# A transformer-like layer step in one kernel: the norm ahead of the feed-forward takes its scale and bias after the turn

## The chip, the cores and the metric

One core of one Trainium2 chip runs the whole layer as one program. The metric is the device time of that program in microseconds (us). The core has a matrix engine (PE in the profile, its weight loads PEld), a vector engine (DVE), a scalar engine (ACT), a general engine (POOL) and a queue engine for transfers (SP). Each runs its own list of instructions in the listed order; an instruction that waits holds all that stand behind it on its engine.

## The reference

One layer on 640 rows (512 prompt rows and 8 x 16 rows of running streams), width 1024. What matters here is its second half: the merged branches go through `w_out`, a norm follows, then a gated feed-forward of width 2816, then a second norm. Everything is fp32.

```python
def layer_norm(x, g, b):
    mu = x.mean(-1, keepdims=True)
    var = jnp.square(x - mu).mean(-1, keepdims=True)
    return (x - mu) * lax.rsqrt(var + LN_EPS) * g + b

z = x @ w_in                      # 1024 -> 6656: branch inputs, query, and three sigmoid gates
...                               # branches A (recurrence), B (conv), C (attention)
merged = g[:, :, 0] * out_a + g[:, :, 1] * out_b + g[:, :, 2] * out_c
x = layer_norm(DEEPNORM_ALPHA * x + merged @ w_out, ln1_g, ln1_b)
ffn = (jax.nn.silu(x @ w_ffn_gate) * (x @ w_ffn_up)) @ w_ffn_down
x = layer_norm(DEEPNORM_ALPHA * x + ffn, ln2_g, ln2_b)
```

## The kernel before, in words

**Split products.** Every fp32 operand of a matmul is kept as a high and a low part (fp32r). ACT copies the high part (`copy`), DVE subtracts it for the low part, and three matmuls (high x high, high x low, low x high) make one product. A row of activations is held turned, 128 features on the partitions and 640 tokens along the row: `xh` and `xl`, 8 blocks of 128 features each. A matmul of 128x320 takes half of the tokens (`HT` = 320, c = 0 or 1), so one full block column costs 8 x 3 x 2 matmuls.

**Order.** The program is a list of `Step`s, one for each weight block, in the order in which PE works through them. For a step, `prep_hi` (ACT) and `prep_lo` (DVE) prepare its weights two to four steps ahead, in the buffers `wh` and `wl` (three each), from `wr` (two buffers of 1 MB, filled by SP). Other work is written as generators ("streams"). A planner (`advance`) adds prices of instructions up per engine and lets a stream issue its next piece whenever DVE and ACT are behind PE by these prices; `finish` forces a stream to its end. `flush` issues the evacuation of the step before. All of this happens when the program is built: what comes out is one fixed order per engine.

**Seven products instead of eight.** The three gates and the feed-forward (except its first 256 columns) are made with Strassen's scheme in Winograd's form, over pairs of column blocks: `seven` issues m1, m4, m2, m6, m5, m7, m3 for the first pair (`first=True`). m1, m2 and m4 read quarters of `xh`/`xl` themselves; m6, m5, m7 and m3 read sums of quarters, s2, s1, s3, s4 in that order. `sums_stream` makes them: it first rebuilds whole fp32 quarters, `xh + xl` (8 adds of 128x640 on DVE in all), mixes them (8 adds or subtractions), and splits each sum in a high and a low part (8 copies on ACT, 8 subtractions on DVE). Its order is s2, s3, s1, s4 for the feed-forward. For the gates s1 comes last and overwrites a quarter of `xh`/`xl`. m2 adds to the PSUM tile of m1, so it cannot start before ACT has copied m1 out. Ahead of m1 of the first pair, `sums_there` issues everything of the sums that is still left.

**w_out and the norm.** `wo_tile` multiplies tiles of 128 tokens (t = 0 to 4), tiles 0 and 1 together, then 2, 3, 4, each 8 x 6 matmuls of 128x512. `wo_evac` then adds the residual (DVE) and starts a stream `x1_t`:

```python
def x1_stream(t):
    yield from ln_rows(res[t], gb["1"][0], gb["1"][1])
    ...                      # the finished rows go to the DRAM scratch x1, for the second residual
    yield from to_xt(t, res[t])
```

`ln_rows` takes the statistics (two BN_STATS), has POOL make the root `rs`, and applies mean, gain, root and bias with four DVE passes of 128x512 per tile. The gain and bias are broadcast over 128 partitions (`gb["1"]`, four 256 KB loads). `to_xt` turns the tile on PE (8 transposes into a PSUM tile `pv`), and ACT and DVE split it from PSUM into `xh` and `xl`.

**Feed-forward start.** Its first 256 columns (gate g and up u, two blocks each) are a `group`: PE first does the c = 0 halves of g0, g1, u0, for which tiles 0, 1 and half of 2 are enough, then `x1_done` forces the streams of the norm to their end and starts the stream of the sums; then come the c = 1 halves, then u1, then the first pair.

**Down.** `before_down` loads the rows of x1 back (`xres`, in the place of `xh`) and the second norm's gain and bias (`gb2`, in the place of `xl`) on POOL's queue. `w_ffn_down` is multiplied for tiles 0 to 2 in 22 steps, then for tiles 3 and 4 in a second round.

## Time and profile before

| what | value |
|---|---|
| runs | 1071.85, 1073.41, 1075.06 us (median 1073.41) |
| profiled execution | 1074.25 us, of it span 1072.1 us |
| mean granted clock of the matrix engine | 0.991 |
| PE busy, share of the span | 1047.4 us, 98% |
| DVE, ACT, POOL busy | 798.8, 469.1, 89.5 us |

All arithmetic on DVE, ACT and PE is recorded by one helper, so its line is always L64; groups are told apart by the names of tiles. `s` is any of the 128x640 slots in SBUF, `pu` and `pv` are PSUM tiles, `x` is the scratch of x1 rows. In a timeline a row gives start, duration, engine, what it writes and reads, and in brackets how long the engine was idle before it and what released it. Matmuls overlap: one of 128x320 is shown with about 310 ns, but the next starts 147 ns later.

### The profile page before, as it was taken

Reading aid. Unit: us, or ns where it says so; the run is one execution under the profiler, and the core shown is the slowest. Engines: PE = TensorE matmul, PEld = TensorE weight load, DVE = VectorE, ACT = ScalarE, POOL = GpSimd, SP = SyncE. Lnnn points to the kernel's source line nnn. Section 1 sums busy time; section 2 is a strip of 40 time slices with the busy share of each in tenths; the row PEclk is TensorE's granted clock in tenths of the full one; section 3 lists DMA queues with packets and bytes.
Section 4 is the critical chain, followed back from the end, with each engine's and each line's share of the span. In section 5 each row is a group of like instructions: output and inputs, shape, how many; then the busy total and the mean of one; then the engine's idle time right before and its main releaser. Section 6 shows DMA issues by size and latency. Waiting matters only on the chain.

```text
span 1072.1 us, 16734 instructions
## 1 busy us (share of the span) xinstructions
PE 1047.4 (98%) x6745; PEld 998.4 (93%) x6745; DVE 798.8 (75%) x1357; ACT 469.1 (44%) x823; POOL 89.5 (8%) x142
## 2 busy tenths in 40 slices
PE   9899999999999999999999998999999999999997
PEld 8799899999999999999998898999999999888886
DVE  7939889799676645989654688888878887544775
ACT  5322655254675438565332024343444444344341
POOL 0100304322100000000001310000000000100111
PEclk9899999999999999999999999999999999999999
DMA  9722126532122122212335321222222222733471
GB/s 346 280 87 80 48 86 209 186 106 79 40 79 79 60 79 79 79 45 80 118 105 193 112 102 40 79 79 82 108 87 80 79 80 85 288 137 139 172 279 40
DMA packets 28541, 123.63 MB, mean 115 GB/s; under 512 B 3728, under 2 KB 4560, under 8 KB 18608
## 3 DMA queue, kind: packets, MB, share of 16 engines
q1 hardware_dynamic: 21744, 100.62, 26.3%
q0 software_dynamic: 6720, 21.94, 6.0%
q8 instruction: 53, 0.87, 0.3%
q14 instruction: 24, 0.20, 0.1%
HBM read 112.67 MB, written 9.88 MB: 114 GB/s over the span
## 4 chain that ended last, share of the span: by engine, by line
PE 83%; DVE 10%; DMA 3%; ACT 2%; issue 1%; POOL 0%; SPq 0%; DVEq 0%; POOLq 0%; ACTq 0%
PE pu L64 74%; PE pv L64 10%; DVE s L64 7%; DVE wl L64 2%; ACT s L64 1%; DMA s<-in_w_mem_k 1%; DMA pb<-in_rows_b 1%; DMA s<-in_x_prompt 1%; DMA s<-in_w_mem_v 1%; DVE xres L64 0%; DVE xl L64 0%; ACT L64 0%; DVE mx L64 0%; POOL s L777 0%; DVE nm L64 0%
## 5 line engine op out<-in xcount | busy, mean ns | idle before, releaser
L64 PE MATMUL pu<-xh,wh 128*128 128x320 f32 x1040 | 251.7, 314 | 8.3 <-ACT s L64 7.5
L64 PE MATMUL pu<-xh,wl 128*128 128x320 f32 x1040 | 247.6, 310 | 0.0
L64 ACT ACTIVATE wh<-wr 128x1024 fp32r<-128x1024 f32 (+1 forms) x149 | 135.1, 908 | 242.2 <-PE pu L64 152.4
L64 PE MATMUL pu<-xl,wh 128*128 128x320 f32 x888 | 220.6, 312 | 4.2 <-DVE xl L64 4.2
L64 PEld LDWEIGHTS pu<-xh,wh 128*128 128x128 f32 x1040 | 178.8, 190 | 12.9 <-ACT s L64 9.2
L64 PE MATMUL pu<-s,wh 128*128 128x320 f32 x1064 | 185.6, 310 | 1.7 <-DVE s L64 1.3
L64 DVE TENSOR_TENSOR s<-s,s 128x640 fp32r<-128x640 f32 (+4 forms) x180 | 129.0, 732 | 67.3 <-ACT s L64 60.7
L64 PEld LDWEIGHTS pu<-xh,wl 128*128 128x128 f32 x1040 | 178.2, 189 | 0.0
L64 DVE TENSOR_TENSOR wl<-wr,wh 128x1024 fp32r<-128x1024 f32 (+1 forms) x113 | 129.9, 1151 | 62.9 <-ACT wh L64 62.7
L64 PEld LDWEIGHTS pu<-s,wh 128*128 128x128 f32 x1064 | 163.1, 188 | 3.3 <-ACT wh L64 1.1
L64 PEld LDWEIGHTS pu<-xl,wh 128*128 128x128 f32 x888 | 155.1, 190 | 4.8 <-DVE xl L64 4.7
L64 PE MATMUL pu<-s,wl 128*128 128x320 f32 x808 | 148.1, 311 | 0.2 <-DVE s L64 0.2
L64 DVE TENSOR_TENSOR s<-s,pu 128x320 f32<-128x320 f32 x188 | 88.5, 485 | 75.0 <-PE pu L64 71.4
L64 ACT ACTIVATE s<-s 128x640 fp32r<-128x640 f32 (+4 forms) x148 | 89.8, 627 | 99.0 <-DVE s L64 97.6
L64 PEld LDWEIGHTS pu<-s,wl 128*128 128x128 f32 x808 | 126.8, 190 | 0.5 <-ACT wh L64 0.5
L64 DVE SCALAR_TENSOR_TENSOR s<-s,pb,s 128x511 f32<-128x511 f32 (+14 forms) x240 | 114.5, 549 | 9.5 <-ACT s L64 9.4
L64 PE MATMUL pu<-wh,s 128*128 128x512 f32 (+1 forms) x396 | 114.8, 383 | 0.0
L64 PEld LDWEIGHTS pu<-wh,s 128*128 128x128 f32 x396 | 72.8, 188 | 13.9
L64 ACT ACTIVATE s<-pu 128x320 f32<-128x320 f32 (+2 forms) x90 | 36.6, 441 | 71.9 <-PE pu L64 71.9
L64 PE MATMUL pu<-wl,s 128*128 128x512 f32 (+1 forms) x198 | 61.6, 383 | 0.4 <-DVE wl L64 0.4
L64 PE MATMUL pv<-wh,s 128*128 128x512 f32 (+1 forms) x152 | 48.7, 367 | 0.4 <-DVE xres L64 0.4
L64 PE MATMUL pu<-s,s 128*128 128x512 f32 (+1 forms) x204 | 46.6, 380 | 0.0
(125 smaller groups left out, 1115.9 us busy)
## 6 DMA issues: line engine op xcount, KB each, us to landing
wr<-in_w_in SPq DMA_DIRECT2D x26, 1024.0 KB, 4.8
wr<-in_w_ffn_down SPq DMA_DIRECT2D x19, 1024.0 KB, 4.8
wr<-in_w_ffn_gate SPq DMA_DIRECT2D x11, 1024.0 KB, 4.8
wr<-in_w_ffn_up SPq DMA_DIRECT2D x11, 1024.0 KB, 4.8
s<-in_cache_k POOLq DMA_DIRECT2D x16, 256.0 KB, 5.2
s<-in_cache_v POOLq DMA_DIRECT2D x16, 256.0 KB, 4.9
wr<-in_proj_a SPq DMA_DIRECT2D x4, 1024.0 KB, 4.8
wr<-in_w_out SPq DMA_DIRECT2D x4, 1024.0 KB, 6.2
```

Source lines behind the costliest of these rows:

```text
L64: return f(*a, **k)
```

## The change: what it does

Mean and root of the norm are still applied to the rows. ACT does it with two passes per tile (scale `rs`, bias `shift`); for the last tile DVE takes one of the two. The rows in x1 are therefore without gain and bias. The tile is then turned, and gain and bias are applied as the eviction from PSUM, where they are one number per partition (columns 43 and 44 of `pa`, which is loaded at the start): half of the blocks on ACT, half on DVE. The result goes into fp32 tiles `whole_x` in SBUF, and `turn_parts` splits it from there into `xh` and `xl`. The `whole_x` tiles are handed to `sums_stream` (`given`), which does not rebuild quarters any more. For the second residual `scale_stream` applies gain and bias to the rows after they are loaded back, with ten DVE passes of 128x1024 at fixed steps of the down stage; `gb2` has two more loads.

The pieces of the norm are no stream any more: `x1_jobs` is a table that names after which matmul group (tile or group, number) each piece is issued. The sums for the feed-forward come in the order s2, s1, s3, s4, and `sums_for` forces, ahead of each product that reads a sum, only what is needed for that one, for the gates too.

```diff
-    it = one.tile([128, 128], I32, name="it")
+    it = get([128, 128], I32)
...
-    def sums_there():
+    def sums_for(n):
         flush()
         for item in list(streams):
             if item[0][:4] == "sums":
-                for _ in item[1]:
-                    pass
-                streams.remove(item)
+                while n not in made:
+                    next(item[1], None)
...
         def whole(n, i):
             t0, k0 = QUARTERS[n]
+            if given is not None:
+                a[n, i] = given.pop((t0 // HT, (k0 + i) // 2))
+                return
...
-        yield from part("s3", "21")
         if in_place is None:
             yield from part("s1", "22")
+        yield from part("s3", "21")
...
-            if first and i == 0:
-                before = sums_there
+            if first and xn[0] == "s":
+                before = lambda xn=xn: sums_for(xn)
...
+    def x1_sum(t):
+        residual(t, wo_acc.pop(t))
+        x1_norm[t] = ln_stats(res[t])
+
+    def x1_scale(t):
+        y = res[t]
+        mv, ve, rs = x1_norm.pop(t)
+        if t < 4:
+            ln_scale(y, mv, rs)
+        else:
+            V.tensor_scalar(y[0], y[0], mv[:, 0:1], rs, op0=OP.subtract, op1=OP.mult)
+            ln_scale(y[1:], mv, rs)
...                                   # both halves of the rows go to the scratch x1 on POOL's queue
+    def x1_gain(t, half):
...
+                    if half:
+                        V.tensor_scalar(w[:, e], src, pa[:, k, 43:44], pa[:, k, 44:45], op0=OP.mult, op1=OP.add)
+                    else:
+                        A.activation(w[:, e], src, AF.Identity, scale=pa[:, k, 43:44], bias=pa[:, k, 44:45])
...
+               (3, 5): [(x1_turn, 2)], (3, 6): [(x1_gain, 2, 0)],
+               (4, 0): [(x1_sum, 3), (x1_gain, 2, 1)], (4, 1): [(x1_scale, 3), (x1_split, 2)], (4, 4): [(x1_turn, 3)],
+               (4, 5): [(x1_gain, 3, 0), (x1_gain, 3, 1), (x1_split, 3)],
+               (5, 0): [(x1_sum, 4), (x1_scale, 4)], (5, 7): [(x1_turn, 4)],
+               (5, 8): [(x1_gain, 4, 0), (x1_gain, 4, 1), (x1_split, 4)]}
...
+    def turn_parts(t, i):
+        for c, a, b in pieces(t):
+            w = whole_x[c, i][:, :, a - c * HT:b - c * HT]
+            copy(xh[:, 2 * i:2 * i + 2, a:b], w)
+            V.tensor_sub(xl[:, 2 * i:2 * i + 2, a:b], w, f32(xh[:, 2 * i:2 * i + 2, a:b]))
...
+        for i, z in ((2, ln1_g), (3, ln1_b), (0, ln2_g), (1, ln2_b)):
...
+        def scale_stream():
+            for t in range(5):
+                for i, op in ((2, OP.mult), (3, OP.add)):
+                    while state["i"] < first["down"] + 2 * t + i + 4:
+                        yield None
+                    V.tensor_tensor(r[:, t], r[:, t], g[:, i], op=op)
+                    yield 1
```

One more slot is there (53), and the rotation of slot numbers shifts by it everywhere. PE has the same matmuls and 40 transposes; four of the five tiles are now turned before the feed-forward begins, not three.

**DVE from the residual of tile 3 on** (SCALAR_TENSOR_TENSOR with `pu` is the residual, `wl` are low parts of the weights of g0 and g1, `s_378_6480` and its like after the change are `whole_x` tiles). Before, from the second half of the residual of tile 3 to the first half of that of tile 4:

```order
L64 SCALAR_TENSOR_TENSOR s_371_6334<-s_371_6334,pu 128x512
L64 TENSOR_TENSOR wl<-wr,wh 128x1024 x2
L64 TENSOR_TENSOR xl<-pv,xh 128x4x128 x2
L64 BN_STATS st<-s_370_6333 128x6
L64 BN_STATS st<-s_371_6334 128x6
L64 BN_AGGR mv<-st 128x2
L64 TENSOR_SCALAR ve<-mv 128x1
L64 SCALAR_TENSOR_TENSOR s_370_6333<-s_370_6333,mv,s_352_6074 128x512
L64 SCALAR_TENSOR_TENSOR s_371_6334<-s_371_6334,mv,s_353_6075 128x512
L64 SCALAR_TENSOR_TENSOR s_370_6333<-s_370_6333,rs,s_354_6078 128x512
L64 SCALAR_TENSOR_TENSOR s_371_6334<-s_371_6334,rs,s_355_6079 128x512
L64 SCALAR_TENSOR_TENSOR s_372_6430<-s_372_6430,pu 128x512
```

After, from the statistics of tile 3 to its shift, and then from the weights to the residual of tile 4:

```order
L64 BN_AGGR mv<-st 128x2
L64 TENSOR_SCALAR ve<-mv 128x1
L64 TENSOR_SCALAR s_369_6315<-pv,pa 128x64 x2
L64 TENSOR_SCALAR s_377_6475<-pv,pa 128x64 x2
L64 TENSOR_SCALAR s_370_6318<-pv,pa 128x64 x2
L64 TENSOR_SCALAR s_378_6480<-pv,pa 128x64 x2
L64 SCALAR_TENSOR_TENSOR shift<-mv,rs 128x1
```

```order
L64 TENSOR_TENSOR wl<-wr,wh 128x1024 x2
L64 TENSOR_SCALAR s_377_6475<-pv,pa 128x128 x2
L64 TENSOR_SCALAR s_378_6480<-pv,pa 128x128 x2
L64 TENSOR_TENSOR xl<-s_373_6436,xh 128x2x128
L64 TENSOR_TENSOR xl<-s_374_6441,xh 128x2x128
L64 TENSOR_TENSOR xl<-s_377_6475,xh 128x2x128
L64 TENSOR_TENSOR xl<-s_378_6480,xh 128x2x128
L64 SCALAR_TENSOR_TENSOR s_375_6469<-s_375_6469,pu 128x512
```

The four full passes with gain and bias are gone from DVE. Eight small gains of tile 2 stand ahead of tile 3's shift, on which ACT's scale of tile 3 waits. The weights' low parts, and the gains and low parts of tile 3, stand ahead of tile 4's residual.

**ACT at the first pair of the feed-forward** (`s<-s` of 128x640 are high parts of the sums; the only copy from `pu` here is m1's). Before:

```order
L64 ACTIVATE s_396_6821<-s_377_6677 128x640
L64 ACTIVATE s_400_6831<-s_398_6825 128x640
L64 ACTIVATE s_402_6835<-s_399_6828 128x640
L64 ACTIVATE wl<-s_381_6703 128x512
L64 ACTIVATE s_404_6864<-pu 128x320
```

After:

```order
L64 ACTIVATE s_397_6887<-s_369_6315 128x640
L64 ACTIVATE wh<-wr 128x512
L64 ACTIVATE s_399_6902<-s_370_6318 128x640
L64 ACTIVATE wl<-s_385_6780 128x512
L64 ACTIVATE s_401_6924<-pu 128x320
```

The copy of m1 stands behind the last two high parts (s4) in both; between these two the weights of m2 now stand.

**ACT at the first pair of the gates** (`xh<-s` are the two halves of s1, the first `s<-pu` of 128x320 alone is m1's copy, `s<-pu,pa` the sigmoid of m2). Before:

```order
L64 ACTIVATE xh<-s_252_4627 128x2x320
L64 ACTIVATE xh<-s_256_4700 128x2x320
L64 ACTIVATE wl<-s_262_4836 128x512
L64 ACTIVATE s_282_5025<-pu 128x320
L64 ACTIVATE wh<-s_263_4838 128x512
L64 ACTIVATE wl<-s_261_4834 128x512
L64 ACT_TABLE_LOAD
L64 ACTIVATE s_288_5067<-pu,pa 128x320
L64 ACTIVATE wh<-wr 128x512
```

After:

```order
L64 ACTIVATE wl<-s_263_4836 128x512
L64 ACTIVATE xh<-s_253_4627 128x2x320
L64 ACTIVATE s_283_5023<-pu 128x320
L64 ACTIVATE wh<-s_264_4838 128x512
L64 ACTIVATE wl<-s_262_4834 128x512
L64 ACT_TABLE_LOAD
L64 ACTIVATE s_289_5056<-pu,pa 128x320
L64 ACTIVATE wh<-wr 128x512
L64 ACTIVATE xh<-s_257_4700 128x2x320
```

The first half of s1 now comes behind m6's weights, and the second half behind the table load and the sigmoid of m2.

## Prediction

> **What bounds the kernel now.** I read the page's share of each engine first, then the waits of the matrix engine, then the timelines around each wait that the change can reach.

> ```profile
> span 1072.1 us, 16734 instructions
> PE 1047.4 (98%) x6745; PEld 998.4 (93%) x6745; DVE 798.8 (75%) x1357; ACT 469.1 (44%) x823; POOL 89.5 (8%) x142
> ...
> PE pu L64 <- ACT s L64: 8.0, 5, 4.3
> ```

> PE is busy for 98% of the span, so the change, which leaves PE's matmuls as they are, can only win what PE stands still or runs at a low clock. The last row is from PE's waits (total, count, longest): one wait of 4.3 us, for a scalar-engine copy. PE's timeline shows it in the first pair of the feed-forward:

> ```profile
> 659.57 0.31 PE L64 MATMUL pu<-xh,wh 128*128 128x320 f32 x1
> ...
> 662.50 0.75 PE L64 MATMUL pu<-xh,wl 128*128 128x320 f32 x4
> 667.57 0.63 PE L64 MATMUL pu<-xh,wh 128*128 128x320 f32 x1 [4.32 <-ACT s L64]
> ...
> 673.90 1.92 PE L64 MATMUL pu<-s,wh 128*128 128x320 f32 x12
> ```

> m1 starts at 659.57; m4 ends with the four matmuls of the second row, 662.50 + 4 x 0.147 = 663.09. m2 should start there and starts at 667.57. What it waited for stands in ACT's and DVE's timelines:

> ```profile
> 656.02 1.98 ACT L64 ACTIVATE s<-s 128x640 fp32r<-128x640 f32 x3
> ...
> 664.35 0.74 ACT L64 ACTIVATE s<-s 128x640 fp32r<-128x640 f32 x1 [6.35 <-DVE s L64]
> 665.94 0.74 ACT L64 ACTIVATE s<-s 128x640 fp32r<-128x640 f32 x1 [0.85 <-DVE s L64]
> ...
> 667.10 0.42 ACT L64 ACTIVATE s<-pu 128x320 f32<-128x320 f32 x1
> ...
> 660.43 2.29 DVE L64 TENSOR_TENSOR s<-s,s 128x640 fp32r<-128x640 f32 x3
> ```

> ACT's copy of m1 (667.10) stands behind the two high parts of s4 (664.35, 665.94), and those wait for DVE, which is still at sums and low parts. The bound here is DVE's queue of sums.

> The wait has a second price. In these windows the columns are the window, its length, busy time (and count) of PE, PEld, DVE, ACT and POOL, the granted clock, the DMA share and GB/s:

> ```profile
> 668.00:673.00 5.00, 5.00 (x20) 5.00 (x20) 4.44 (x8) 2.38 (x6) 0.00 (x0) 0.50 0.00 0
> ...
> 470.00:474.00 4.00, 4.00 (x29) 4.00 (x29) 3.97 (x8) 2.87 (x5) 0.00 (x0) 1.00 0.00 0
> ...
> 39.81 0.63 PE L64 MATMUL pu<-xl,wh 128*128 128x320 f32 x1 [3.35 <-DVE xl L64]
> 41.00:43.00 2.00, 2.00 (x9) 2.00 (x9) 1.90 (x4) 0.00 (x0) 0.00 (x0) 0.50 0.80 279
> ```

> After the wait the clock is 0.50. m2 and m6 are 24 matmuls at 0.147 = 3.52 us at full clock, but m5 starts 6.33 us after m2. So the stall costs 673.90 - (663.09 + 3.52) = 7.29 us: 4.48 of waiting (the row's 4.32 and the gap beside it) and 2.81 of half clock. A wait of 3.35 us elsewhere also leaves the clock at 0.50; the gates' wait of 0.53 (below) leaves it at 1.00.

> **Sums by need and given quarters.** The rows of the groups (busy time in us and mean ns behind the bar) of the stretch from 592 to 670:

> ```profile
> L64 DVE TENSOR_TENSOR s<-xh,xl 128x640 f32<-128x640 f32 x8 | 6.4, 819 | 0.0
> L64 DVE SCALAR_TENSOR_TENSOR s<-s,rs,s 128x512 f32<-128x512 f32 x10 | 7.0, 745 | 0.0
> L64 DVE SCALAR_TENSOR_TENSOR s<-s,mv,s 128x512 f32<-128x512 f32 x10 | 7.0, 744 | 0.0
> L456 POOL TENSOR_TENSOR rs<-ve,mhalf 128x1 f32<-128x1 f32 x5 | 4.9, 977 | 44.6 <-DVE ve L64 44.6
> ```

> The eight adds that rebuild quarters go: 6.4 us of exactly the queue that m2 waits for. If everything else kept its place, m1's copy would move from 667.10 to 660.7, before m1 itself is through, and the wait would be gone.

> Everything else does not keep its place, so I also lay the queue out by hand, with start-to-start prices: 0.76 for 128x640 on DVE (2.29 for three, above), 0.66 on ACT (1.98 for three). From 641.8, when the last `xl` is written: six mixes to 646.5; the low part of s2 waits for ACT, which is held by u1's weights until g0's buffers are free (645.5), and with u1's low part and the rest of s2 DVE is at 650.9; the mixed quarters of s1 and s3 to 653.7; m1's low weights and the low parts of s1 and s3 to 657.9; then a mix, u0's evacuation and m4's low weights to 660.0; a mix and s4's low parts to 662.3; u1's evacuation and m2's low weights to 663.7. Those are needed at about 664.5 (the low weights are the last third of a product), and the copy of m1, on ACT from 662.1 to 662.5, at 663.1. So PE does not wait, with a slack of 0.6 us. **-7.3 us**, the whole loss.

> **Norm at fixed points, turned gain.** Full passes with gain and bias were 14.0 us of DVE in this stretch; they leave it. New are scale passes on ACT and gains at the eviction. The nearest rows of the whole run:

> ```profile
> L64 ACT ACTIVATE xres<-xres,shift,rs 128x512 f32<-128x512 f32 x1 | 0.8, 817 | 13.5 <-DVE shift L64 13.5
> L64 ACT ACTIVATE s<-pv 128x128 fp32r<-128x128 f32 x4 | 0.8, 269 | 0.0
> L64 DVE TENSOR_TENSOR s<-s,pv 128x128 f32<-128x128 f32 x8 | 2.2, 278 | 0.0
> L64 DVE TENSOR_SCALAR ve<-mv 128x1 f32<-128x1 f32 x15 | 2.3, 154 | 0.5
> L64 DVE TENSOR_SCALAR nm<-mx 128x4 f32<-128x4 f32 x5 | 2.1, 427 | 0.2
> ```

> A gain on DVE is bounded by 154 ns (one column) and 427 (the dearest small pass with one operand); I take 278, the row of the same shape from PSUM. At 427 the eight gains of tile 2, which stand ahead of tile 3's shift, cost 8 x 0.15 = 1.2 more there, and the turns of tiles 3 and 4 wait for 1.9 us together. At 154 nothing is won, since PE does not wait there.

> The turns stand at fixed points in PE's order now, so each is a new place where PE can wait:

> ```profile
> 598.41 6.96 PE L64 MATMUL pu<-s,s 128*128 128x512 f32 x30
> ...
> 629.65 0.31 PE L64 MATMUL pu<-xh,wh 128*128 128x320 f32 x1
> ...
> 641.97 0.31 PE L64 MATMUL pu<-xh,wh 128*128 128x320 f32 x1
> ...
> 629.62 1.29 DVE L64 SCALAR_TENSOR_TENSOR s<-s,pu 128x512 f32<-128x512 f32 x2
> 632.38 0.15 DVE L64 TENSOR_SCALAR ve<-mv 128x1 f32<-128x1 f32 x1
> ```

> Six matmuls of the output product are 1.36 us (6.80 for 30, start to start). By that tile 2 ends at 606.1, tile 3 at 618.7, tile 4 at 630.5. Residual and statistics take 2.9 us (629.62 to 632.53), the root about 1.0 on POOL, the two scale passes 1.5. Tile 3: sum, root, then the shift behind tile 2's gains; scaled at 625.0, turned at 625.5. Tile 4: behind the low parts of g0's and g1's weights and tile 3's gains and low parts DVE is through with the residual and statistics at 635.2; one half of the rows is scaled on DVE, the other on ACT until 638.05; the turn is placed at 637.6, its second half at 638.0. The earlier turns have over 1.7 us to spare (ready at 600.7, 602.2, 613.0 for 602.5, 607.4, 615.1). g0's low weights are through at 629 and needed at 630.8. The c = 1 halves come at 642.0 as before; tile 4's last `xl` is written between 640.6 and 641.8. Two points without slack (turn 4, this `xl`) I book at **+0.5 us**.

> The residual loads of POOL's queue now stand behind the roots of tiles 0 and 1, which puts the load of tile 2 at about 606.4, 0.3 after that tile ends, ahead of a turn with 2 us to spare: no cost. The slot, the two columns of `pa` and the four loads of 256 KB that fall away lie beside PE's work and cost nothing.

> **Gates.** Here the need-order puts s1's second half behind m2's sigmoid and its table load:

> ```profile
> 469.75 0.41 PE L64 MATMUL pu<-xh,wh 128*128 128x320 f32 x1 [0.53 <-ACT s L64]
> ...
> 475.52 1.99 PE L64 MATMUL pu<-s,wl 128*128 128x320 f32 x12 [0.23 <-DVE s L64]
> ...
> 471.86 1.28 ACT L64 ACT_TABLE_LOAD   x1 [1.12 <-PE pu L64]
> 473.15 0.53 ACT L64 ACTIVATE s<-pu,pa 128x320 f32<-128x320 f32 x1
> ```

> Before, PE loses 0.70 at m2 (469.05 to 469.75) and 0.39 at m7 (475.13 to 475.52). After: m2 at 469.05, its end 1.76 later releases the table load (471.06 to 472.34), sigmoid to 472.8, m7's weights to 473.3, s1's second half on ACT to 474.0 and on DVE to 474.9. m5, due at 472.6, needs that at 473.3 and so waits about 1.55; m7 starts at 475.9. **+0.4 us.**

> **Second residual in the down stage.** Ten more DVE passes and two broadcast loads of 512 KB:

> ```profile
> 936.40 1.22 DVE L64 TENSOR_TENSOR wl<-wr,wh 128x1024 fp32r<-128x1024 f32 x1
> 939.74 0.83 DVE L64 TENSOR_TENSOR s<-s,s 128x640 fp32r<-128x640 f32 x1 [2.12 <-ACT s L64]
> ...
> 915.65 0.53 POOL L1666 DMA_DIRECT2D gb<-in_ln_g  x1
> ...
> gb<-in_ln_g POOLq DMA_DIRECT2D x1, 512.0 KB, 13.8
> gb<-in_ln_b POOLq DMA_DIRECT2D x1, 512.0 KB, 14.9
> 910.00:930.00 20.00, 20.00 (x98) 17.13 (x97) 12.81 (x16) 6.75 (x8) 3.70 (x7) 1.00 0.91 340
> ```

> A step of three tiles is 3 x 1.36 = 4.08 us of PE, and DVE is idle for 2.12 of them; a pass of 1.22 fits. The first is placed six steps into the stage, near 938; the loads landed at 929.5 before, and 1 MB more at 340 GB/s is 3 us. Hidden: 0. Without that cover (DVE held by a load) the low weights behind it have some 3.7 us before PE stops.

> **Sum.** -7.3 + 0.5 + 0.4 = -6.4. The profiled execution took 1074.25 us, 0.84 above the median of the runs, 1073.41; so 1067.85 against that one and 1067.0 against the median.

> [...] The rows leave open what a new wait between 0.70 and 3.35 us does to the clock. [...]

> **Rivals.**
> 1. Part of the stall stays: the queue of sums ends 2 to 4 us later than I lay it out. For it: the slack is 0.6 and every wait of ACT for DVE and back adds. Each us past it costs one, and past some 3 the half clock comes too: 1068.5 to 1073. Chance 0.14.
> 2. New waits at turns 3 and 4 or at g0's weights, 2 to 3 us, with or without 2.7 of half clock: 1069.5 to 1072.2. For it: slacks of 0.5 and 0. Against it: 278 rather than 427 as the price of a gain. Chance 0.12.
> 3. The gates' wait of 1.55 already halves the clock: 1067.0 + 2.8 = 1069.8. Against it: the wait of 0.53 did nothing. Chance 0.04.
> 4. Slower: DVE waits in the down stage for the broadcast gain and the low weights queue behind it. PE stops if the gain lands after about 941.6; to undo 6.4 and lose 3.2 more, with 2.7 of half clock, it must land at 948.5, 32 us after its issue where 14.9 was measured: over 1076.6. Chance 0.08.

> **How the numbers follow.** The stall gone, 1065.5 to 1069, has 0.62: predicted 1067.0. The range reaches down by the 0.5 booked, the 0.4 of the gates and the spread of the runs, and up over the first three cases: 1064.8 to 1073.2. A measurement of this kernel can tell 0.3%, 3.2 us, from no change. Faster: the forecast whole, most of the third rival and the low halves of the first two, 0.75; the same: the rest of these, 0.17; slower: 0.08.

> **What would show it.** Right: in the first pair of the feed-forward no wait of PE over 1 us and a clock of 1.00; the adds from `xh` and `xl` halved in count, the remaining eight in the gates; in the gates' first pair a wait of about 1.5 for DVE's `xl` with the clock still 1.00; turns with waits under 1 us; ten passes on `xres` beside a busy PE. Wrong: a wait on ACT or DVE in the feed-forward's first pair, PE waiting for ACT's rows at turns 3 or 4, gains dearer than 0.43 us, or DVE standing for `gb` in the down stage.

## The result, and the profile after

| | runs | median us | lowest to highest |
|---|---|---|---|
| before | 4 | 1073.35 | 1071.85 to 1075.06 |
| changed | 4 | 1067.40 | 1066.40 to 1068.33 |

The ratio is 0.9944 (95% interval 0.9927 to 0.9961): 6.0 us faster, 1067.4 where 1067.0 was forecast. A later comparison on one chip gave 0.9944 again (0.9930 to 0.9957, 5 rounds, median 1067.31).

The first lines of the changed kernel's page:

```profile
span 1066.6 us, 16778 instructions
PE 1045.3 (98%) x6745; PEld 996.2 (93%) x6745; DVE 799.8 (75%) x1383; ACT 486.0 (46%) x870; POOL 86.1 (8%) x140
```

Two rows of PE's waits in the same kernel (total us, count, longest):

```profile
PE pu L64 <- DVE xl L64: 4.6, 3, 3.3
PE pu L64 <- ACT s L64: 3.1, 3, 2.4
```

DVE has as much to do as before (799.8 us against 798.8): eight adds of 6.4 us and the four passes per tile with gain and bias are gone, ten passes of the second residual, the gains and one half-row scale have come. What changed is where it does it. The wait of 4.3 us for ACT has left the list (8.0 us in five waits before, 3.1 in three now). The first pair of the feed-forward, in PE's timeline:

```profile
664.25 0.75 PE L64 MATMUL pu<-xh,wl 128*128 128x320 f32 x4
664.84 0.31 PE L64 MATMUL pu<-xh,wh 128*128 128x320 f32 x1
...
666.01 0.75 PE L64 MATMUL pu<-xh,wh 128*128 128x320 f32 x4
666.60 1.92 PE L64 MATMUL pu<-s,wl 128*128 128x320 f32 x12
668.35 1.92 PE L64 MATMUL pu<-s,wh 128*128 128x320 f32 x12
```

m2 starts at 664.84, 0.147 after the last start of m4: no wait. m6 follows at 666.60 and m5 at 668.35, 1.76 apart (12 x 0.147), and the window below has the clock at 1.00. ACT's timeline there, and its last row DVE's:

```profile
660.20 0.74 ACT L64 ACTIVATE s<-s 128x640 fp32r<-128x640 f32 x1 [1.95 <-DVE s L64]
...
662.33 0.74 ACT L64 ACTIVATE s<-s 128x640 fp32r<-128x640 f32 x1 [0.87 <-DVE s L64]
...
663.50 0.41 ACT L64 ACTIVATE s<-pu 128x320 f32<-128x320 f32 x1
...
664.64 0.69 DVE L64 TENSOR_TENSOR wh<-wr,wh 128x512 fp32r<-128x512 f32 x1
```

A window (columns as in the prediction) over the place that ran at 0.50 before:

```profile
665.00:670.00 5.00, 5.00 (x37) 5.00 (x35) 4.96 (x10) 2.00 (x4) 0.00 (x0) 1.00 0.00 0
```

The copy of m1 (663.50) still stands behind both high parts of s4 and these still wait for DVE, but it ends 0.9 us before m2 wants it; the low weights of m2 (DVE, 664.64 to 665.33) are there 0.7 before their first use at 666.01. The stall is not gone by a wide margin; the queue of sums now ends just ahead of PE. All PE matmuls but the transposes stand in the same order in both kernels, so the traces can be lined up matmul by matmul, and the later or earlier start of the same matmul shows where the time went:

| stretch | booked | measured |
|---|---|---|
| until 135 us, which the change hardly touches | 0 | +1.1 |
| first pair of the gates | +0.4 | +0.6 |
| turns and start of the feed-forward | +0.5 | +0.1 |
| first pair of the feed-forward | -7.3 | -7.3 |
| all that follows | 0 | 0.0 |
| span | -6.4 | -5.5 (1072.1 to 1066.6) |

The 1.1 us at the start are scatter of one execution; without them the trace gives -6.6, the medians give -6.0. The trace's record of the granted clock has stretches of 0.50 near 40 and 131 us (38.73 to 45.55 and 130.89 to 134.30 in the kernel before, 39.98 to 46.80 and 132.14 to 135.55 in the changed one), and they are not there in every execution of the same work: the one with two adds put back (below) has none of them and is 4.5 us earlier than the changed kernel behind them, 3.7 of it from the places of the two stretches (2.2 and 1.5). A second profile of the changed kernel lies 0.5 us below the first ahead of the gates' m5. Single runs of one kernel, which differ by 2 us and more, go the same way: of the 15 runs of the kernel before that stand beside the adds below, the fastest (1071.19 us) has a mean clock of 0.995, the slowest (1075.33) one of 0.991.

### The profile page after: what moved, and what is told of

It reads as the page before. It is cut to its first block, busy times and chain, and to the rows that moved or that the text cites. A ratio compares the mean times of both kernels' runs of the same rounds, so it can differ in the third digit from the quotient of the medians.

```text
span 1066.6 us, 16778 instructions
## 1 busy us (share of the span) xinstructions
PE 1045.3 (98%) x6745; PEld 996.2 (93%) x6745; DVE 799.8 (75%) x1383; ACT 486.0 (46%) x870; POOL 86.1 (8%) x140
## 4 chain that ended last, share of the span: by engine, by line
PE 84%; DVE 10%; DMA 3%; ACT 2%; issue 1%; POOL 0%; SPq 0%; DVEq 0%; ACTq 0%; POOLq 0%
PE pu L64 74%; PE pv L64 10%; DVE s L64 6%; DVE wl L64 2%; ACT s L64 1%; DMA s<-in_w_mem_k 1%; DMA s<-in_x_prompt 1%; DMA pb<-in_rows_b 1%; ACT L64 1%; DMA s<-in_w_mem_v 1%; DVE xres L64 0%; DVE mx L64 0%; DVE xl L64 0%; POOL s L781 0%; ACT wh L64 0%
## 5 line engine op out<-in xcount | busy, mean ns | idle before, releaser
L64 PE MATMUL pu<-xh,wh 128*128 128x320 f32 x1040 | 250.2, 313 | 4.2 <-ACT s L64 2.6
L64 PE MATMUL pu<-xh,wl 128*128 128x320 f32 x1040 | 247.5, 311 | 0.1
L64 ACT ACTIVATE wh<-wr 128x1024 fp32r<-128x1024 f32 (+1 forms) x149 | 135.0, 908 | 233.9 <-PE pu L64 141.1
L64 PE MATMUL pu<-xl,wh 128*128 128x320 f32 x888 | 220.1, 311 | 4.6 <-DVE xl L64 4.6
L64 PE MATMUL pu<-s,wh 128*128 128x320 f32 x1064 | 185.4, 310 | 1.8 <-DVE s L64 1.3
L64 PEld LDWEIGHTS pu<-xh,wh 128*128 128x128 f32 x1040 | 177.9, 190 | 8.5 <-ACT s L64 3.7
L64 PEld LDWEIGHTS pu<-xh,wl 128*128 128x128 f32 x1040 | 178.5, 190 | 0.3 <-ACT s L64 0.3
L64 DVE TENSOR_TENSOR wl<-wr,wh 128x1024 fp32r<-128x1024 f32 (+1 forms) x113 | 129.8, 1151 | 59.6 <-ACT wh L64 59.4
L64 DVE TENSOR_TENSOR s<-s,s 128x640 fp32r<-128x640 f32 (+4 forms) x180 | 128.8, 733 | 53.6 <-ACT s L64 51.5
L64 PEld LDWEIGHTS pu<-s,wh 128*128 128x128 f32 x1064 | 163.1, 188 | 3.2 <-ACT wh L64 1.1
L64 PEld LDWEIGHTS pu<-xl,wh 128*128 128x128 f32 x888 | 154.6, 190 | 5.4 <-DVE xl L64 5.4
L64 PE MATMUL pu<-s,wl 128*128 128x320 f32 x808 | 146.6, 309 | 0.0
L64 DVE TENSOR_TENSOR s<-s,pu 128x320 f32<-128x320 f32 x188 | 88.4, 484 | 72.1 <-PE pu L64 68.5
L64 ACT ACTIVATE s<-s 128x640 fp32r<-128x640 f32 (+4 forms) x148 | 90.0, 627 | 91.2 <-DVE s L64 90.0
L64 PEld LDWEIGHTS pu<-s,wl 128*128 128x128 f32 x808 | 125.5, 188 | 0.2 <-issue 0.2
L64 DVE SCALAR_TENSOR_TENSOR s<-s,pb,s 128x511 f32<-128x511 f32 (+14 forms) x240 | 114.5, 550 | 9.4 <-ACT s L64 9.4
L64 PE MATMUL pu<-wh,s 128*128 128x512 f32 (+1 forms) x396 | 114.6, 382 | 0.0
L64 PEld LDWEIGHTS pu<-wh,s 128*128 128x128 f32 x396 | 72.9, 188 | 14.1
L64 ACT ACTIVATE s<-pu 128x320 f32<-128x320 f32 (+2 forms) x90 | 36.6, 440 | 66.7 <-PE pu L64 66.7
L64 PE MATMUL pu<-wl,s 128*128 128x512 f32 (+1 forms) x198 | 61.6, 383 | 0.8 <-DVE wl L64 0.8
L64 PE MATMUL pv<-wh,s 128*128 128x512 f32 (+1 forms) x152 | 48.7, 367 | 0.4 <-DVE xres L64 0.4
L64 PE MATMUL pu<-s,s 128*128 128x512 f32 (+1 forms) x204 | 47.2, 382 | 0.0
```

Source lines behind the costliest of these rows:

```text
L64: return f(*a, **k)
```

## Experiments

Medians and ratios are against runs of the kernel before on the same chip. "Lined up" means how much later the same matmuls start behind the place of the edit, less how much later they start ahead of it; the scatter at the start of the program is left out by that. It compares one execution of each kernel.

**Adds put back, two, four and eight.** The sums take the kept tiles, but DVE rebuilds some of them first, outside the planner's prices, so that nothing else moves:

```diff
                 a[n, i] = given.pop((t0 // HT, (k0 + i) // 2))
+                if len(given) >= 6:
+                    V.engine.tensor_tensor(a[n, i], *(f32(x[:, k0 + i:k0 + i + 2, t0:t0 + HT]) for x in (xh, xl)), op=OP.add)
```

With 6 these are the first two adds, with 4 in its place the first four, with 0 all eight.

> The changed kernel with two of the eight adds of 128x640 put back on DVE at the head of the sums (they write the same numbers over the kept tiles; every other instruction stays in its order). Theory, that m2 waits for DVE's queue of sums: m1's copy at 663.5 and m2's low weights at 665.3 move by 2 x 0.78 = 1.6 us against slacks of 0.7 to 0.9, so m2 waits 0.7 to 0.9 us, the clock stays at 1.00, and the time is 1068.2 us (1067.6 to 1068.8). Rival, that the order by need carries the gain: no wait over 0.3 us, 1067.4. Rival, that any wait near 1 us halves the clock: 1071.

> As before with four adds put back. Theory: 3.1 us more, a wait of 2.2 to 2.5 us at m2. This tells what a wait between 0.70 and 3.35 us does to the clock: with the clock kept 1069.8 us, with the half clock of some 2.8 us 1072.5. Rival, the order by need: 1067.4 to 1068.

> All eight adds put back, everything else as in the changed kernel (norm at fixed points, gain after the turn, order by need). Theory: 6.3 us more, a wait of 5.4 to 5.7 at m2 and 2.8 of half clock, 1075.5 us (1074.5 to 1076.5), which is above the kernel before, since the sums now start later. Rival, that order and norm carry the gain: 1067.4 to 1069.

| adds | median us | ratio (95%) | lined up with the changed kernel |
|---|---|---|---|
| 2 | 1067.60 | 0.9941 (0.9925 to 0.9957) | +1.2 |
| 4 | 1069.77 | 0.9963 (0.9948 to 0.9978) | +3.4 |
| 8 | 1073.55 | 0.9997 (0.9987 to 1.0006) | +6.6 |

PE's timeline with two adds, with four, and with eight:

```profile
660.67 0.42 PE L64 MATMUL pu<-xh,wh 128*128 128x320 f32 x1 [0.18 <-ACT s L64]
...
666.91 1.99 PE L64 MATMUL pu<-s,wl 128*128 128x320 f32 x12 [0.24 <-DVE s L64]
```

```profile
663.06 0.41 PE L64 MATMUL pu<-xh,wh 128*128 128x320 f32 x1 [1.48 <-ACT s L64]
```

```profile
654.61 0.56 PE L64 MATMUL pu<-xh,wl 128*128 128x320 f32 x2 [1.10 <-DVE wl L64]
...
665.24 0.86 PE L64 MATMUL pu<-xh,wl 128*128 128x320 f32 x4 [0.97 <-DVE wl L64]
668.44 0.42 PE L64 MATMUL pu<-xh,wh 128*128 128x320 f32 x1 [2.35 <-ACT s L64]
```

Windows behind the last wait, with four adds and with eight:

```profile
664.00:667.00 3.00, 3.00 (x13) 3.00 (x13) 2.96 (x6) 0.95 (x4) 0.00 (x0) 0.50 0.00 0
```

```profile
670.00:672.50 2.50, 2.50 (x11) 2.50 (x11) 2.46 (x5) 1.17 (x3) 0.00 (x0) 0.50 0.00 0
```

The stall comes back add by add. Two adds cost 1.2 lined up (0.8 expected), with the clock kept; in the times this can't be told from the changed kernel (0.9941 against 0.9944). Four wait 1.8 us from the end of m4 (1.48 in the row's brackets), less than the 2.2 expected, and in the profiled execution the clock is already at 0.50 after it, for 3.4 us that cost 1.5; so the median falls on the figure for a kept clock, and only the window shows that it was not kept there. With all eight back, the rest of the change (norm on turned rows, fixed points, order by need) is worth nothing that can be measured: 0.9997. My figure for this run was 2 us too high: the delay came as three waits (u1's, m4's low weights, then m2), and behind the last of them the clock was halved for 3.4 us, not 6.8.

**The old order of the sums, adds gone.** Feed-forward only:

```diff
-            if first and xn[0] == "s":
+            if first and i == 0 and how:
+                before = sums_all
+            elif first and xn[0] == "s" and not how:
                 before = lambda xn=xn: sums_for(xn)
```

`how` is set for the feed-forward alone, `sums_all` issues all that is left of the sums ahead of m1, and the order is s2, s3, s1, s4 again (not shown).

> The changed kernel with the adds gone, but the sums of the feed-forward in the old order s2, s3, s1, s4 and all of them forced ahead of m1. Theory, the adds: DVE has the same work before m2, only weights of m4 and u1's evacuation change places with it; at most 1 us lost, 1067.0 to 1068.5 us. Rival, the order by need carries the gain: a wait of 3 to 4.5 us at m2 or m4 and the half clock are back, 1072 to 1075.

1067.35 us, ratio 0.9939 (0.9924 to 0.9954); lined up, the pair ends 0.15 us earlier than in the changed kernel, and PE does not wait there. The order by need carries nothing of the gain.

**The order by need alone, in the kernel before.** Order s2, s1, s3, s4 and forcing by need, with the adds and the old norm:

```diff
-            if first and i == 0:
-                before = sums_there
+            if first and xn[0] == "s":
+                before = lambda xn=xn: sums_for(xn)
```

> The kernel before with one part of the change alone: the sums in the order s2, s1, s3, s4 and forced by need, in the gates and in the feed-forward; adds, norm and second residual stay as before. Theory, that the order wins nothing: the wait at m2 of the feed-forward keeps 3.5 to 4.5 us with its half clock, and the gates lose 0.6 us more, 1073.9 us (1073 to 1075). Rival, that the order by need shortens the wait when the adds are there: 1 to 3 us off the wait, 1070 to 1072.5.

1074.12 us, ratio 1.0009 (0.9999 to 1.0018). The time came as expected, but the wait did not stay where I put it. PE's timeline:

```profile
673.75 0.63 PE L64 MATMUL pu<-s,wh 128*128 128x320 f32 x1 [3.40 <-ACT s L64]
675.31 3.30 PE L64 MATMUL pu<-s,wh 128*128 128x320 f32 x11 [0.93 <-DVE s L64]
```

m2 to m7 run without a wait (lined up, m5 starts 7.3 us earlier than before), and m3, the last product, then waits 3.40 and 0.93 for s4 and runs at half clock as well (0.50 in the window from 675 to 679). The seven are done 0.5 us earlier than before, lined up, and the gates lose 0.7. DVE's work up to s4 is what counts; an order by need only chooses the product that waits for the end of it.

**Gates.** The changed kernel again, then with the gates' sums forced as before, then with the second half of s1 ahead of m2:

```diff
             elif first and i == 2 and following:
-                before = lambda: (following.sums_1(), following.sums_2())
+                before = lambda: (following.sums_1(), following.sums_2(), how and sums_for("s1"))
```

> The changed kernel itself again, as the measure for the other three. All theories: 1067.4 us as before, within 1 us, and in its trace waits of 0.7 and 0.5 us at m5 of the gates' first pair.

> The changed kernel with the gates' sums forced all at once ahead of m1, as in the kernel before; the feed-forward keeps its order. Theory, that the order by need costs 0.6 us in the gates: PE loses 0.8 at m2 and 0.4 at m7 again in place of 1.5 to 1.9 at m5, the time 0.6 below the changed kernel's, 1066.8. Rival, that the order by need helps the gates: 0.5 us above it, 1067.9.

> The changed kernel with the second half of the gates' s1 forced ahead of m2, so that its high part on ACT stands behind m1's copy and ahead of the table load of m2's sigmoid. Theory: m2 starts unhindered (m1's copy still stands first) and m5 finds s1 ready; no wait at m2 or m5, some 0.2 to 0.4 at m7 may stay; 1.2 to 1.6 us below the changed kernel in the trace, 1066.0 in time. Rival, that DVE and not the table load holds s1: the wait at m5 stays at 1 us or more, 1067.4.

| | median us of 5 | lowest to highest | ratio to before (95%) | lined up |
|---|---|---|---|---|
| changed | 1067.31 | 1066.25 to 1068.48 | 0.9944 (0.9930 to 0.9957) | |
| gates as before | 1067.16 | 1066.01 to 1067.85 | 0.9942 (0.9930 to 0.9954) | -0.7 |
| s1 early | 1065.32 | 1064.09 to 1066.91 | 0.9926 (0.9913 to 0.9938) | -1.7 |

The changed kernel's PE and ACT, its window over the wait, and then ACT and DVE of the version with s1 early:

```profile
475.09 0.41 PE L64 MATMUL pu<-xh,wh 128*128 128x320 f32 x1 [0.75 <-ACT xh L64]
475.95 0.41 PE L64 MATMUL pu<-xl,wh 128*128 128x320 f32 x1 [0.45 <-DVE xl L64]
...
472.07 1.28 ACT L64 ACT_TABLE_LOAD   x1 [2.09 <-PE pu L64]
...
474.32 0.72 ACT L64 ACTIVATE xh<-s 128x640 fp32r<-128x640 f32 x1
```

```profile
474.00:479.00 5.00, 3.80 (x25) 3.31 (x24) 3.04 (x5) 2.08 (x4) 0.00 (x0) 1.00 0.25 72
```

```profile
468.06 0.73 ACT L64 ACTIVATE xh<-s 128x640 fp32r<-128x640 f32 x1
...
470.77 1.28 ACT L64 ACT_TABLE_LOAD   x1 [1.46 <-PE pu L64]
...
471.12 0.82 DVE L64 TENSOR_TENSOR xl<-s,xh 128x640 fp32r<-128x640 f32 x1
```

The window has the clock at 1.00 with PE standing 1.2 us. In the changed kernel the second high part of s1 (474.32) stands behind the table load, and m5 waits for it on ACT (0.75) and on DVE (0.45). Ahead of the table load it is done by 468.8, in time that ACT stood idle, and PE has no wait left in this pair. With the sums as before the waits at m2 and m7 are back (0.54 and 0.24 in the rows' brackets), and the gates are 0.7 us cheaper than in the changed kernel lined up, which the times alone could not tell. The version with s1 early is the fastest of all: 1065.32 us, 0.7% below the kernel before and 2.0 us below the changed one by the medians (1.7 lined up).

**The second residual without its distance.** The ten passes six steps earlier:

```diff
-                    while state["i"] < first["down"] + 2 * t + i + 4:
+                    while state["i"] < first["down"] + 2 * t + i - 2:
```

> The changed kernel with the ten passes of the second residual issued six steps earlier, from the start of the down stage. Theory, that only their place keeps them hidden: the first pass stands on DVE at about 913 and waits for the broadcast gain until 923 to 926; the low parts behind it are needed at about 920.6, so PE waits 4 to 6 us and then loses 1.5 to 2.8 at half clock, 1073 to 1076. Rival, that low parts are prepared far enough ahead: at most 1 us, 1067.4 to 1068.4.

1073.97 us, ratio 1.0003 (0.9993 to 1.0013). DVE's and PE's timelines, and a window behind the wait:

```profile
918.93 1.23 DVE L64 TENSOR_TENSOR xres<-xres,gb 128x1024 f32<-128x1024 f32 x1 [7.93 <-DMA gb<-in_ln_g]
...
924.27 1.22 PE L64 MATMUL pu<-wl,s 128*128 128x512 f32 x2 [4.94 <-DVE wl L64]
```

```profile
925.00:929.00 4.00, 4.00 (x11) 3.13 (x10) 4.00 (x4) 0.00 (x0) 0.00 (x0) 0.50 0.69 262
```

DVE stands 7.93 us for the broadcast gain, the low weights behind it come late, and PE waits 4.94 and then runs at half clock until 929.25 (the record has 0.50 from 922.42, 6.8 us in all): +7.5 lined up, the whole gain of the change. The mechanism of the fourth rival is real, and only the place of the passes keeps it away.

**Dearer gains ahead of a fixed turn.** DVE's eight gains of tile 2 issued twice:

```diff
                         V.tensor_scalar(w[:, e], src, pa[:, k, 43:44], pa[:, k, 44:45], ...)
+                        if t == 2:
+                            V.engine.tensor_scalar(w[:, e], src, pa[:, k, 43:44], pa[:, k, 44:45], ...)
```

> The changed kernel with DVE's eight gains of tile 2 issued twice (the same numbers again), which puts 8 x 0.25 = 2.0 us ahead of tile 3's shift. Theory of the second rival, that a fixed turn has no cover: ACT's scale of tile 3 ends at 628.9 in place of 626.9, the turn placed at 627.2 waits 1.7 us, and the time is 1069.1 us, or 1070.6 if the clock halves for one stretch. Rival, that the wait is made up again before the feed-forward's first pair, where DVE and ACT set the pace: under 0.7 us, 1067.4 to 1068.

1070.02 us, ratio 0.9959 (0.9945 to 0.9973); lined up +3.9. PE's timeline, and a window behind the wait:

```profile
627.92 1.78 PE L64 MATMUL pv<-ident,s 128*128 128x128 f32 x8 [1.94 <-ACT s L64]
```

```profile
629.00:632.00 3.00, 3.00 (x10) 2.48 (x9) 2.36 (x9) 3.00 (x9) 0.41 (x1) 0.50 0.45 175
```

A delay of 2.0 us on DVE is a wait of 1.94 at the turn, and as much again is lost behind it: from the turn's start to the next matmul 1.43 us pass (0.79 in the changed kernel), since ACT's second pass ends only at 628.58 and the clock is at 0.50 (the window), and the 18 matmuls after it take 5.49 (4.18). Nothing downstream makes it up. The profiled execution (1070.91) is one of the two slowest of five, though, and the median is only 2.7 above the changed kernel's, so whether the half clock comes in every execution is not shown.

## Why the prediction was right

**The stall.** The reading of the four queues held: m2 waited for m1's copy, this for the high parts of s4, these for DVE's sums. The copy by my hand-laid queue ends at 662.5, in the time scale of the kernel before; in the trace it ends at 663.91, where that execution lies 1.75 us behind (1.1 from its start, 0.6 from the gates), so at 662.2. m2's low weights: 663.7 forecast, 663.6 in the trace. All 7.3 us were won because the queue ends in time, if only by 0.7 us; the run with two adds shows the edge.

The heading under which I booked it, sums by need and given quarters, gives one of its two halves too much: the given quarters are the whole of it, the order by need is worth nothing in the feed-forward and costs in the gates.

**The norm and its turns.** I booked 0.5 us and 0.1 was lost. The rows at the two points that I called without slack:

```profile
625.40 1.52 ACT L64 ACTIVATE s<-s,shift,rs 128x512 f32<-128x512 f32 x2 [5.07 <-DVE shift L64]
...
627.20 1.03 PE L64 MATMUL pv<-ident,s 128*128 128x128 f32 x8
...
638.83 0.82 ACT L64 ACTIVATE s<-s,shift,rs 128x512 f32<-128x512 f32 x1 [4.22 <-DVE shift L64]
...
639.21 1.14 PE L64 MATMUL pv<-ident,s 128*128 128x128 f32 x8
```

Tile 3 is scaled at 626.92 for a turn at 627.20, 0.3 to spare (0.5 forecast). Turn 4 runs 0.11 longer than turn 3, which is the wait for its second half (639.65). The price of a gain was mis-sized. The groups, busy us and mean ns:

```profile
L64 ACT ACTIVATE s<-pv,pa 128x128 f32<-128x128 f32 x16 | 6.0, 454 | 4.2 <-PE pv L64 4.2
L64 DVE TENSOR_SCALAR s<-pv,pa 128x128 f32<-128x128 f32 x16 | 5.5, 404 | 7.7 <-ACT s L64 7.7
...
L64 DVE TENSOR_SCALAR s<-pv,pa 128x64 f32<-128x64 f32 x8 | 2.1, 333 | 0.0
L64 DVE TENSOR_TENSOR xres<-xres,gb 128x1024 f32<-128x1024 f32 x10 | 12.2, 1218 | 0.0
```

404 and 333 ns on DVE, not 278, though inside the bounds. It did no harm since in a queue the spacing counts: eight of 128x64 took 2.10 us from first start to last end, 0.25 from start to start. The profiled execution with the gains doubled puts the second rival's price at 3.9 us for 2.0 of delay, so this term was right by 0.3 us of slack.

**Gates.** +0.4 booked, +0.6 measured: the mechanism (table load and sigmoid ahead of s1) was as described, and the clock stayed at 1.00, so the third rival did not come. The wait came as two pieces, for ACT and for DVE, 1.2 us together in the brackets; lined up, m5 loses 1.5, where 1.55 was forecast. So the two small terms missed in opposite directions, by 0.4 and 0.2.

**Down.** Ten passes of 1.218 us beside a busy PE, at no cost. The first gain landed 12.7 us after its issue at 909.29, at 922.0, and the first pass starts at 934.91.

**The half clock.** What a wait between 0.70 and 3.35 us does was open, and the runs answer it, not as I leaned: the "some 3" of the first rival was my estimate from the wait of 3.35, and a wait of 1.48 was already followed by the half clock. Each stretch of half clock here is 3.4 or 6.8 us long, but for the one that the end of the program cuts off (from 1069.55 in the kernel before, from 1063.98 in the changed one). The waits are those in the rows' brackets:

| wait of PE, us | half clock after it |
|---|---|
| 0.18 and 0.24 (two adds), 0.75 and 0.45 (gates) | none |
| 1.48 (four adds), 1.94 (gains twice), 2.35 (eight adds) | 3.4 us |
| 4.32 (before), 4.94 (passes early), 3.40 and 0.93 (order alone) | 6.8 us |
| 3.35 (before) and 3.34 (changed) at 40 us | 6.8 us |
| 3.38 (two adds) at 40 us, the same wait | none |
| 2.45 (before) and 2.40 (changed) at 130 us | 3.4 us |
| 2.40 (two adds) at 128 us, the same wait | none |

In the kernel before the clock changes at 38.73, 45.55, 130.89, 134.30, 666.78, 673.60 and 1069.55 us, in the changed one at 39.98, 46.80, 132.14, 135.55 and 1063.98. Within each of these two traces all changes lie whole multiples of the same 3.4133 us apart, to within 0.02 ((1069.55 - 38.73) / 302). Against the program they lie differently: the first drop comes 2.59 us after the start of the matmul ahead of the wait near 40 us (36.14) in the kernel before, 2.82 after it (37.16) in the changed one. Here are windows of that length, laid on each trace's changes of the clock. First, those that end where the clock drops: in the kernel before, in the changed kernel again, with four adds. Then three that end with the clock kept: two near 40 us with two adds, and the changed kernel's gates.

```profile
35.31:38.73 3.42, 1.14 (x6) 0.68 (x4) 3.35 (x6) 2.62 (x5) 1.48 (x1) 1.00 0.78 301
...
36.45:39.86 3.41, 0.06 (x1) 0.00 (x0) 3.34 (x7) 2.79 (x5) 1.48 (x1) 1.00 0.32 121
...
660.35:663.76 3.41, 1.92 (x12) 1.40 (x11) 3.34 (x7) 2.54 (x6) 0.00 (x0) 1.00 0.00 0
...
35.17:38.59 3.42, 1.50 (x7) 0.97 (x6) 3.35 (x7) 2.25 (x5) 1.40 (x1) 1.00 0.80 308
38.59:42.00 3.41, 1.95 (x13) 1.95 (x14) 3.41 (x6) 0.81 (x1) 0.07 (x1) 1.00 0.49 69
...
473.47:476.88 3.41, 2.21 (x13) 1.72 (x13) 2.54 (x5) 2.61 (x5) 0.00 (x0) 1.00 0.00 0
```

PE is busy for 1.14, 0.06 and 1.92 us of the windows that are followed by the half clock, and for 1.50, 1.95 and 2.21 of those that are not. The same wait near 40 us fills one window of the changed kernel again, and is shared between two with two adds, where the clock stays. So the length of a wait does not decide alone (3.35 and 3.38, 2.40 and 2.40 went both ways), and PE's busy time in such a window does not either (1.92 lost the clock, 1.50 kept it); what decides is not shown.

No run shows the 2.7 us of half clock that the second and the fourth rival add: behind waits of 1.48 to 2.35 us 1.5 to 2.0 us were lost, 2.4 with the passes early (7.5 lined up, 5.1 of it from the end of the matmul before), 2.81 in the kernel before. Of the waits of 1.48 to 2.45 us in the table five of six were followed by the half clock, so a new wait of 2 to 3 us at the turns would more likely have given the upper end of the second rival, 1072, than the lower.

## What to carry to other kernels

When PE waits at a product, follow the release back through every queue to the engine that is really behind, and count its work up to the last thing that any near product needs: taking work out of that queue won here, while reordering by need alone only moved the wait to a later product. Lay the new queue out by hand with start-to-start prices and look at what is left as slack, since 0.3 to 0.7 us here were the difference between all and part of the gain. An instruction forced "just ahead of its reader" may land behind something long on another engine, here a table load of 1.28 us; put it where that engine stands idle.
